# Six shared gather buffers and three raw weight buffers instead of five and four, in a two-layer hybrid trunk with product-key experts

## The chip, the cores and the metric

The kernel runs on one core of one Trainium2 chip. The metric is the device time of one execution in microseconds (us). A core has five engines that run at the same time, each with its own list of instructions in a fixed order: TensorE (PE) does matrix products, VectorE (DVE) and ScalarE (ACT) do elementwise work, GpSimd (POOL) issues the gathers, and SyncE (SP) issues nearly all plain transfers. An instruction that waits holds up all that stand behind it on its engine.

## The reference

Two layers work on 512 latent tokens and 256 context tokens of width 1024. Cut to what matters:

```python
for l in range(DEPTH):                      # 2
    p, pc = h @ w_in[l], hc @ w_in[l]       # latent, context
    ml_c, state = _mlstm_branch(pc, ...)    # context scan first
    ml_x, _ = _mlstm_branch(p, ..., state)  # its state starts the latent scan
    x = x + mod[2] * _mixer_merge(p, ml_x, ...)
    x = x + mod[5] * _peer(h, w_q, keys, u_tab, v_tab)
    # the context stream likewise, in layer 0 only

def _peer(h, ...):      # per token: 8 heads x 16 = 128 experts e, weights g
    a = gelu(einsum('nhkd,nd->nhk', u_tab[e], h)) * g
    return einsum('nhk,nhkd->nd', a, v_tab[e])
```

An expert is one row of `u_tab` and one row of `v_tab`, each 1024 numbers, in tables of 16384 rows a layer.

## The kernel before

**Weights.** Every weight tile of 128 x 1024 numbers (512 KB) comes from memory into a raw buffer `wr` (line 298 in `wload`, 817 in `routing`, 1138 in `s_block`). ScalarE casts it to `wh` (L292) and VectorE takes the difference `wl` (L293), after which the raw buffer is free; TensorE then makes three products for each pair (L312). The pool is opened once with `W_MIX`, (4, 3): four raw buffers and three of each part, for the whole kernel. In the context routing of layer 0 the raw tile goes to TensorE directly (L819), with no parts.

**Experts of the latent tokens.** In `peer_lat`, three of four token blocks use all experts as dense products (`s_block` and `dense`, accumulated on L1201). The fourth gathers rows: `gather` takes 128 rows of u and then 128 of v (one row for each of 128 tokens per gather, 512 KB), and VectorE reduces them (L948, L966). A row is read `LAG` rows after its gather was written down. These gathers are also tied to the pace of the dense loop.

**Experts of the context tokens.** In `gather_ctx`, each of four half blocks (64 tokens) takes 64 rows of u, reduced by VectorE on L1027, and 64 gathers of v, two for a step, whose products TensorE makes on L1061; these steps run one step behind their gathers (`VLAG`). A half block of v also holds one buffer for a matrix `dg` of its weights (L1055). The half blocks are spread as background work over the latent mixer of layer 0 (u of half 0, then v of half 0 with u of half 1 in alternation, then u of half 2), the routing of `peer_lat` of layer 0 (v of halves 1 and 2), and the start of layer 1 (u and v of half 3).

**Buffers of the rows.** All gathered rows use the tag `gat` with `GB` buffers (five), except the rows of u in the latent mixer of layer 0, which have a pool of their own, `ug`, with `UB` (three) and the distance `ULAG` (two). Three staging tiles of the context routing and the results also pass through `gat`. `rows` (line 916 on) picks the pool by its argument `own`.

**Order.** A background list hands out one row for so many microseconds of foreground work (`tick`). A scheduler then fixes each engine's order from its own estimate of when an instruction's inputs and buffers are ready, so a change in buffers also moves instructions that have nothing to do with gathers.

Of the kernel before, what the change touches and what calls it, by code (L numbers as in the profile page):

```python
# [47 lines left out]
V_COST, PS_C = 0.6, (3, 2)  # L48
NFT = 4
ND = 3  # L50
W_MIX = (4, 3)
NADA, ADA_RATE, ADA_RATE2 = 4, 0.3, 0.8
VB = 4
LAG = 3
COST_T = (2.0, 4.0)
GB = 5
UB, ULAG, VLAG = 3, 2, 1
GTB, VRB, GRB, GSB = 2, 2, 2, 2
AB, AHEAD = 3, 3

# [1 line left out]
def build(nc, tc, I, out):  # L62
# [126 lines left out]
    def mk(p, shape, dt=F32, tag=None, bufs=None):  # L189
        nid[0] += 1  # L190
        kw = {} if bufs is None else {"bufs": bufs}
        return p.tile(list(shape), dt, name=f"{tag}_{nid[0]}", tag=tag, **kw)

    def psum(tag="mm", n=None):
        p, t, bufs = pspool[tag]
        return mk(p, [128, 512], F32, t, bufs)
# [718 lines left out]
    def rows(tab, ix, own=False):  # L915
        t = mk(pu[0], [128, D], F32, "ug", UB) if own else mk(pg[0], [128, D], F32, "gat", GB)
        d = G.indirect_dma_start(out=t, out_offset=None, in_=tab, in_offset=bass.IndirectOffsetOnAxis(ap=ix, axis=0))  # L917
        if gate[0] is not None:
            tc.add_manual_dep(d.ins, gate[0].ins.name, SYNC, reason="spread the gathers over the loop")
        return t  # L920

    def gather(l, h, b, i12, gw, mod, s):
# [17 lines left out]
        def u_rows():  # L940
            ts = {}
            for j in range(128 + LAG):
                if j < 128:
                    ts[j] = rows(u_tab, eu[:, j:j + 1])
                if j >= LAG:
                    i = j - LAG
                    t = ts.pop(i)
# [6 lines left out]
        def v_rows(x):  # L954
            ts = {}
            on = mk(pg[0], [128, D], F32, "hn", 1)
            for j in range(128 + LAG):
                if j < 128:
                    ts[j] = rows(v_tab, eu[:, j:j + 1])
                if j >= LAG:  # L960
                    i = j - LAG
                    t = ts.pop(i)
# [14 lines left out]
    def gather_ctx(l, h, b, i12, gw, hnd, ond):  # L977
# [3 lines left out]
        u_tab, v_tab = I["peer_u"], I["peer_v"]  # L981
# [7 lines left out]
        def two(ps, src, c):  # L989

            for p in (0, 64):
                PE.matmul(ps[p:p + 64, :64], ident[:, 64 * c:64 * c + 64], src[:, p:p + 64], start=True, stop=True,
                          tile_position=(0, p))
            return ps[:, :64]

        def half(c):
            t0 = 128 * b + 64 * c
            i = 2 * b + c
            p = (pg[0], pl)[b]
            eu, a, w = (mk(p, [128, 64], dt, n + str(i), 1) for n, dt in (("hu", I32), ("ha", F32), ("hw", F32)))  # L1000
            V.tensor_scalar(eu, two(psum("sm"), ef, c), float(l * 16384), None, op0=ALU.add)
            V.tensor_copy(w, two(psum("sm"), gw, c))
            hn = mk(pg[0], [128, D], F32, "hn" if i == 0 else "gat", 1 if i == 0 else GB)
            for k in range(KT):
                ps = psum("sm")
                for q in (0, 64):
                    PE.matmul(ps[q:q + 64, :128], h[k][0][:, t0:t0 + 64], ident, start=True, stop=True,
                              tile_position=(0, q))
                S.copy(hn[:, 128 * k:128 * k + 128], ps[:, :128])
            if i:  # L1010
                nc.gpsimd.dma_start(hnd[i - 1], hn)

            def u_rows():
                hx = hn
                if i:
                    hx = mk(pg[0], [128, D], F32, "hn", 1)
                    nc.gpsimd.dma_start(hx, hnd[i - 1])
                ts = {}
                own = pu[0] is not None
                lag = ULAG if own else LAG  # L1020
                for j in range(64 + lag):
                    if j < 64:
                        ts[j] = rows(u_tab, eu[:, j:j + 1], own)
                    if j >= lag:
                        n = j - lag
                        t = ts.pop(n)
                        V.scalar_tensor_tensor(t, t, 1.0, hx, op0=ALU.mult, op1=ALU.mult, accum_out=a[:, n:n + 1])  # L1027
                    if j < 64:
                        yield
                S.activation(a, a, AF.Gelu_apprx_tanh)  # L1030
                V.tensor_tensor(a, a, w, ALU.mult)
                ps = psum("acc")
                for q in (0, 64):
                    PE.matmul(ps[q:q + 64, :64], a[q:q + 64, :], ident[q:q + 64, q:q + 64], start=True, stop=True,
                              tile_position=(q, q))
                S.copy(at[:, 64 * c:64 * c + 64], ps[:, :64])

            def v_rows():
                po = psum("acc")
                ts = {}  # L1040
                for p in range(32 + VLAG):
                    if p < 32:
                        ts[p] = []
                        for q in range(2):
                            tok = 64 * c + 32 * q + p
                            ts[p].append(rows(v_tab, ev[:, tok:tok + 1]))
                            if q == 0:
                                yield
                    if p >= VLAG:
                        n = p - VLAG  # L1050
                        rg, r = n // 16, n % 16
                        if r == 0:

                            dg = mk(pg[0], [128, 2, 16, 32], F32, "gat", GB)
                            G.memset(dg, 0.0)  # L1055
                            dd = dg.rearrange("p q r c -> p q (r c)")[:, :, 16 * rg:16 * rg + 15 * 33 + 1:33]
                            V.tensor_copy(dd, at[:, 64 * c:64 * c + 64].rearrange("p (q r) -> p q r", q=2)
                                          [:, :, 16 * rg:16 * rg + 16])
                        t = ts.pop(n)
                        for m in range(4):  # L1060
                            PE.matmul(po[32 * m:32 * m + 32, :], dg[:, m % 2, r, :],  # L1061
                                      t[m % 2][:, 512 * (m // 2):512 * (m // 2) + 512],
                                      start=n == 0, stop=n == 31, tile_position=(0, 32 * m))
                    if p < 32:
                        yield
                on = mk(pg[0], [128, 512], F32, "gat", GB)
                S.copy(on, po)
                nc.gpsimd.dma_start(ond[i], on)

            return u_rows, v_rows  # L1070

        return half(0) + half(1)

    def add_ctx(x, i, src, mod):

        on = mk(pg[0], [128, 512], F32, "gat", GB)
        nc.gpsimd.dma_start(on, src)
# [69 lines left out]
    def dense(l, h, gd, sp, nsp, nb, x, mod):  # L1147
# [62 lines left out]
        for b in range(nb):  # L1210
            on.append(mk(pg[0], [128, D], F32, "gat", GB))
            for half in range(2):
# [52 lines left out]
    def weight_pool(nr=0, ns=0):  # L1265

        pt.close()
        if pw_cm[0]:
            pw_cm[0].__exit__(None, None, None)
            pw_cm[0] = None  # L1270
        if nr:
            pw_cm[0], pw[0] = open_pool("pw", "right")
            pw[1:] = [nr, ns]
            pt.open()
# [13 lines left out]
    def ctx_residual(src):  # L1288
        cm, p = right_pool("xc")
        x = mk(p, [128, KT, CTX], F32, "xc")  # L1290
        nc.sync.dma_start(x, src.rearrange("(k p) t -> p k t", p=128))
        return x, cm
# [32 lines left out]

    weight_pool(*W_MIX)
    xc, xc_cm = ctx_residual(I["ctxT"])
# [246 lines left out]
```

## Time and profile before

| | us |
|---|---|
| three runs | 4578.3, 4589.01, 4588.94 |
| their median | 4588.94 |
| the profiled execution | 4592.53 |
| its span in the trace | 4590.7 |
| TensorE busy in it | 4241.2 |
| TensorE idle in it (4590.7 less 4241.2) | 349.5 |

The profile is of one execution. Around its span lie 1.8 us. It ran 3.6 us longer than the median of the three runs. TensorE's busy time includes time at a lower granted clock; the granted clock is 1.0 at full speed.

### The profile page before, as it was taken

How to read it: one execution, taken by the hardware profiler on the slowest of the kernel's cores; microseconds unless marked ns; L12 is line 12 of the kernel's file. 1: busy time of each engine (PE TensorE's matmuls, PEld its weight loads, DVE VectorE, ACT ScalarE, POOL GpSimd, SP SyncE). 2: the span in 40 equal slices, each digit the busy share in tenths (PEclk: the TensorE clock that was granted, in tenths of full speed). 3: DMA queues.
4: the chain of work that ended last, by engine and by line, in shares of the span. 5: the costliest groups of instructions: out<-in, count | busy, mean ns of one | idle time of the engine just before them, and what ended most of it. 6: DMA issues, size and time to landing. Idle time of an engine off the chain costs nothing.

```text
span 4590.7 us, 61300 instructions
## 1 busy us (share of the span) xinstructions
PE 4241.2 (92%) x22364; PEld 3459.9 (75%) x22364; DVE 3319.5 (72%) x6764; ACT 1628.8 (35%) x2314; POOL 1302.9 (28%) x1061
## 2 busy tenths in 40 slices
PE   7899769987999999999999888989999999999998
PEld 4795545655667799788888764567789998888887
DVE  3854878766578497677777685365699996777775
ACT  3541212322324355333333331243335553333333
POOL 0000346552243331233333354200012322233231
PEclk8999859988999999999999999989999999999999
DMA  7546768986577896999999787512248889898984
GB/s 279 202 152 221 261 210 319 342 282 205 183 271 253 305 344 241 339 323 319 326 333 326 255 288 252 199 60 74 92 151 295 314 297 328 300 313 310 312 313 157
DMA packets 417342, 1187.42 MB, mean 259 GB/s; under 512 B 39440, under 2 KB 142608, under 8 KB 413968
## 3 DMA queue, kind: packets, MB, share of 16 engines
q1 hardware_dynamic: 260992, 631.52, 39.9%
q0 software_dynamic: 150928, 549.52, 33.6%
q8 instruction: 176, 2.88, 0.3%
q10 hardware_dynamic: 5120, 2.47, 0.2%
q14 instruction: 126, 1.03, 0.1%
HBM read 1092.40 MB, written 90.96 MB: 258 GB/s over the span
## 4 chain that ended last, share of the span: by engine, by line
PE 37%; issue 15%; DMA 10%; DVE 9%; POOL 4%; ACT 1%; SPq 0%; POOLq 0%; DVEq 0%; ACTq 0%
PE s L312 11%; PE acc L1201 11%; PE mm L312 9%; POOL gat L917 4%; DMA gsr<-sp 3%; DMA vr<-in_peer_v 2%; DMA gat<-in_peer_v,ev 2%; PE sm L1120 2%; DMA gat<-in_peer_v,eu 1%; DVE gat L948 1%; DMA gat<-in_peer_u,eu 1%; DVE wl L293 1%; DVE vl L293 1%; DVE hn L966 1%; PE acc L1061 1%
## 5 line engine op out<-in xcount | busy, mean ns | idle before, releaser
L292 ACT CAST wh<-wr 128x1024 fp32r<-128x1024 f32 x498 | 521.6, 1048 | 1234.9 <-PE mm L312 706.9
L293 DVE TENSOR_TENSOR wl<-wr,wh 128x1024 fp32r<-128x1024 f32 x498 | 608.0, 1221 | 347.8 <-ACT wh L292 343.0
L312 PE MATMUL s<-hh,wh 128*128 128x384 f32 x2048 | 702.1, 343 | 3.8 <-ACT gs L1144 3.8
L312 PE MATMUL s<-hh,wl 128*128 128x384 f32 x2048 | 694.6, 339 | 5.0 <-DVE wl L293 5.0
L312 PE MATMUL s<-hl,wh 128*128 128x384 f32 x2048 | 693.7, 339 | 0.0
L917 POOL DMA_INDIRECT gat<-in_peer_u,eu x256 | 332.9, 1300 | 1258.5 <-DVE pu L861 468.3
L312 PE MATMUL mm<-hh,wh 128*128 128x512 f32 (+1 forms) x1552 | 592.7, 384 | 42.0 <-DVE sg L787 19.8
L1201 PE MATMUL acc<-vh,al 128*128 128x512 f32 x1536 | 605.2, 394 | 14.0 <-DVE al L293 13.9
L312 PE MATMUL mm<-hh,wl 128*128 128x512 f32 (+1 forms) x1552 | 588.4, 380 | 30.7 <-DVE wl L293 30.5
L1201 PE MATMUL acc<-vl,ah 128*128 128x512 f32 x1536 | 604.7, 394 | 7.7 <-DVE vl L293 7.7
L1201 PE MATMUL acc<-vh,ah 128*128 128x512 f32 x1536 | 602.2, 393 | 10.0 <-ACT vh L292 5.4
L312 PE MATMUL mm<-hl,wh 128*128 128x512 f32 (+1 forms) x1552 | 586.8, 379 | 3.7 <-DVE hl L293 2.3
L917 POOL DMA_INDIRECT gat<-in_peer_v,eu x256 | 335.2, 1309 | 643.8 <-PE acc L1201 485.2
L292 ACT CAST vh<-vr 128x1024 fp32r<-128x1024 f32 x256 | 268.8, 1050 | 545.0 <-DMA vr<-in_peer_v 521.7
L917 POOL DMA_INDIRECT gat<-in_peer_v,ev x256 | 301.7, 1179 | 477.0 <-PE acc L1061 352.4
L312 PEld LDWEIGHTS mm<-hh,wh 128*128 128x128 f32 x1552 | 306.3, 198 | 147.0 <-issue 52.9
L312 PEld LDWEIGHTS s<-hh,wh 128*128 128x128 f32 x2048 | 386.6, 189 | 30.5 <-issue 14.1
L312 PEld LDWEIGHTS s<-hh,wl 128*128 128x128 f32 x2048 | 386.1, 189 | 6.1 <-DVE wl L293 6.0
L966 DVE SCALAR_TENSOR_TENSOR hn<-gat,a,hn 128x1024 f32<-128x1024 f32 x254 | 325.6, 1282 | 89.8 <-DMA gat<-in_peer_v,eu 89.3
L312 PEld LDWEIGHTS s<-hl,wh 128*128 128x128 f32 x2048 | 386.7, 189 | 4.3 <-issue 0.8
L312 PEld LDWEIGHTS mm<-hh,wl 128*128 128x128 f32 x1552 | 306.4, 197 | 110.8 <-DVE wl L293 39.2
L293 DVE TENSOR_TENSOR vl<-vr,vh 128x1024 fp32r<-128x1024 f32 x256 | 313.0, 1223 | 98.6 <-ACT vh L292 98.1
(378 smaller groups left out, 7005.5 us busy)
## 6 DMA issues: line engine op xcount, KB each, us to landing
wr<-in_peer_uT SPq DMA_DIRECT2D x256, 512.0 KB, 5.2
vr<-in_peer_v SPq DMA_DIRECT2D x256, 512.0 KB, 5.9
wr<-in_w_inT SPq DMA_DIRECT2D x134, 512.0 KB, 4.5
wada<-in_w_adaT SPq DMA_DIRECT2D x96, 512.0 KB, 4.5
gd<-gt SPq DMA_DIRECT2D x24, 2048.0 KB, 8.2
gr<-gd SPq DMA_DIRECT2D x64, 768.0 KB, 8.8
sp<-gs SPq DMA_DIRECT2D x78, 384.0 KB, 4.8
gsr<-sp SPq DMA_DIRECT2D x78, 384.0 KB, 6.2
```

Of the source, the lines that this page charges most:

```text
L292: S.copy(hi, src)
L293: V.tensor_tensor(lo, src, hi, ALU.subtract)
L312: PE.matmul(ps, w[k][a], x[k][b], start=first and k == 0 and i == 0, stop=last and k == n - 1 and i == 2)
L917: d = G.indirect_dma_start(out=t, out_offset=None, in_=tab, in_offset=bass.IndirectOffsetOnAxis(ap=ix, axis=0))
L948: V.scalar_tensor_tensor(t, t, 1.0, hn, op0=ALU.mult, op1=ALU.mult, accum_out=a[:, i:i + 1])
L966: V.scalar_tensor_tensor(on, t, a[:, i:i + 1], on, op0=ALU.mult, op1=ALU.add)
L1061: PE.matmul(po[32 * m:32 * m + 32, :], dg[:, m % 2, r, :], t[m % 2][:, 512 * (m // 2):512 * (m // 2) + 512], start=n == 0, stop=n == 31, t ...
L1120: PE.matmul(ps[:, 128 * i:128 * i + 128], o2[:, i].rearrange("p a b -> p (a b)"), o1[:, i, :], start=True, stop=True)
L1201: mm = PE.matmul(acc[b][half], a[p][:, ts], v[q][:, ds], start=done == 0 and n == 0, stop=done == 127 and n == 2)
```

## The change

Five numbers and one condition are changed. The raw weight buffers go from four to three, the buffers of `gat` from five to six (4 KB per partition either way). The distance `LAG` goes from three to four rows, `ULAG` from two to three. In the latent mixer of layer 0, every fourth row of u (index 3, 7, 11 and so on) takes a buffer of `gat`, the other three take the pool `ug` as before.

```diff
--- before.py
+++ after.py
@@ -48,13 +48,13 @@
 V_COST, PS_C = 0.6, (3, 2)
 NFT = 4
 ND = 3
-W_MIX = (4, 3)
+W_MIX = (3, 3)
 NADA, ADA_RATE, ADA_RATE2 = 4, 0.3, 0.8
 VB = 4
-LAG = 3
+LAG = 4
 COST_T = (2.0, 4.0)
-GB = 5
-UB, ULAG, VLAG = 3, 2, 1
+GB = 6
+UB, ULAG, VLAG = 3, 3, 1
 GTB, VRB, GRB, GSB = 2, 2, 2, 2
 AB, AHEAD = 3, 3
 
@@ -1020,7 +1020,7 @@
                 lag = ULAG if own else LAG
                 for j in range(64 + lag):
                     if j < 64:
-                        ts[j] = rows(u_tab, eu[:, j:j + 1], own)
+                        ts[j] = rows(u_tab, eu[:, j:j + 1], own and j % (ULAG + 1) < UB)
                     if j >= lag:
                         n = j - lag
                         t = ts.pop(n)
```

No transfer, product or reduction is added or removed: there are 1065 instructions on GpSimd and 1163 on SyncE in both. What moves is shown below at three places. The number behind a name counts the tiles in program order, and one tile can be a number or two apart in the two kernels; `hu_888` and `hu_902` are the row numbers of u of half blocks 0 and 1, `ev` those of v.

GpSimd in the latent scan of layer 0, before. Every row of u goes in turn through the three `ug` buffers, with the first v rows and the first `dg` between them:

```order
L917 DMA ug_5434<-in_peer_u,hu_888_4613 128x1024
L917 DMA gat_5761<-in_peer_v,ev_885_4608 128x1024
L917 DMA ug_5437<-in_peer_u,hu_888_4613 128x1024
L917 DMA ug_5440<-in_peer_u,hu_888_4613 128x1024
L917 DMA ug_5443<-in_peer_u,hu_888_4613 128x1024
L1055 MEMSET gat_5763 128x1024
L917 DMA ug_5446<-in_peer_u,hu_888_4613 128x1024
L917 DMA ug_5449<-in_peer_u,hu_888_4613 128x1024
L917 DMA ug_5499<-in_peer_u,hu_888_4613 128x1024
L917 DMA ug_5502<-in_peer_u,hu_888_4613 128x1024
L917 DMA ug_5505<-in_peer_u,hu_888_4613 128x1024
L917 DMA ug_5508<-in_peer_u,hu_888_4613 128x1024
```

The same place after:

```order
L917 DMA ug_5436<-in_peer_u,hu_888_4613 128x1024
L917 DMA gat_5501<-in_peer_u,hu_888_4613 128x1024
L917 DMA ug_5439<-in_peer_u,hu_888_4613 128x1024
L917 DMA gat_5513<-in_peer_u,hu_888_4613 128x1024
L917 DMA gat_5564<-in_peer_u,hu_888_4613 128x1024
L917 DMA ug_5445<-in_peer_u,hu_888_4613 128x1024
L917 DMA ug_5448<-in_peer_u,hu_888_4613 128x1024
L917 DMA ug_5498<-in_peer_u,hu_888_4613 128x1024
L917 DMA gat_5623<-in_peer_u,hu_888_4613 128x1024
L917 DMA gat_5635<-in_peer_u,hu_888_4613 128x1024
L917 DMA ug_5504<-in_peer_u,hu_888_4613 128x1024
L917 DMA gat_5686<-in_peer_u,hu_888_4613 128x1024
```

Rows of u in `gat` (5501, 5513, 5564, 5623, 5635, 5686) now stand up to several rows ahead of their turn; the v rows come later.

GpSimd at the start of the alternation of v of half 0 and u of half 1, before:

```order
L917 DMA ug_5758<-in_peer_u,hu_902_4657 128x1024
L917 DMA ug_5809<-in_peer_u,hu_902_4657 128x1024
L917 DMA gat_5812<-in_peer_v,ev_885_4608 128x1024
L917 DMA ug_5814<-in_peer_u,hu_902_4657 128x1024
L917 DMA gat_5817<-in_peer_v,ev_885_4608 128x1024
L917 DMA ug_5823<-in_peer_u,hu_902_4657 128x1024
L917 DMA gat_5826<-in_peer_v,ev_885_4608 128x1024
L917 DMA ug_5890<-in_peer_u,hu_902_4657 128x1024
L917 DMA gat_5893<-in_peer_v,ev_885_4608 128x1024
L917 DMA ug_5899<-in_peer_u,hu_902_4657 128x1024
```

And after:

```order
L917 DMA gat_5808<-in_peer_u,hu_902_4657 128x1024
L917 DMA gat_5811<-in_peer_v,ev_885_4608 128x1024
L917 DMA gat_5816<-in_peer_v,ev_885_4608 128x1024
L917 DMA ug_5813<-in_peer_u,hu_902_4657 128x1024
L917 DMA gat_5825<-in_peer_v,ev_885_4608 128x1024
L917 DMA ug_5822<-in_peer_u,hu_902_4657 128x1024
L917 DMA ug_5889<-in_peer_u,hu_902_4657 128x1024
L917 DMA gat_5892<-in_peer_v,ev_885_4608 128x1024
L917 DMA gat_5898<-in_peer_u,hu_902_4657 128x1024
L917 DMA gat_5901<-in_peer_v,ev_885_4608 128x1024
```

One row of u in four now takes its place among the v rows' buffers.

SyncE in the context routing of layer 0 (`wr` are the raw tiles of the query weights, `wada` those of the modulation of layer 1, which wait for a product of this routing), before:

```order
L817 DMA wr_3634<-in_w_qT 128x1024
L817 DMA wr_3672<-in_w_qT 128x1024
L817 DMA wr_3710<-in_w_qT 128x1024
L248 DMA wada_3606<-in_w_adaT 128x1024
L248 DMA wada_3608<-in_w_adaT 128x1024
L248 DMA wada_3644<-in_w_adaT 128x1024
L248 DMA wada_3646<-in_w_adaT 128x1024
L817 DMA wr_3748<-in_w_qT 128x1024
L817 DMA wr_3786<-in_w_qT 128x1024
L248 DMA wada_3682<-in_w_adaT 128x1024
L248 DMA wada_3684<-in_w_adaT 128x1024
```

And after:

```order
L817 DMA wr_3634<-in_w_qT 128x1024
L817 DMA wr_3672<-in_w_qT 128x1024
L248 DMA wada_3606<-in_w_adaT 128x1024
L248 DMA wada_3608<-in_w_adaT 128x1024
L248 DMA wada_3644<-in_w_adaT 128x1024
L248 DMA wada_3646<-in_w_adaT 128x1024
L817 DMA wr_3710<-in_w_qT 128x1024
L817 DMA wr_3748<-in_w_qT 128x1024
L248 DMA wada_3682<-in_w_adaT 128x1024
L248 DMA wada_3684<-in_w_adaT 128x1024
L817 DMA wr_3786<-in_w_qT 128x1024
```

Each raw tile behind the third now stands one or two `wada` pairs later, since its buffer is that of the tile three before it.

## Rows read from the trace of the kernel before

**Rows 1.** The page: span, and busy time, share and instructions of each engine.

```profile
span 4590.7 us, 61300 instructions
...
PE 4241.2 (92%) x22364; PEld 3459.9 (75%) x22364; DVE 3319.5 (72%) x6764; ACT 1628.8 (35%) x2314; POOL 1302.9 (28%) x1061
```

**Rows 2.** Stage windows: stretch, length, busy (count) per engine, PEclk, DMA share, GB/s.

```profile
560.00:700.00 140.00, 83.46 (x420) 62.98 (x420) 103.99 (x225) 34.74 (x76) 57.70 (x53) 0.62 0.65 210
1380.00:1610.00 230.00, 216.32 (x1303) 175.65 (x1303) 150.38 (x378) 88.64 (x114) 81.63 (x66) 0.96 0.79 281
1800.00:2600.00 800.00, 777.62 (x3716) 677.19 (x3716) 603.65 (x757) 279.38 (x385) 269.08 (x210) 0.99 0.90 317
2760.00:3000.00 240.00, 214.10 (x1035) 132.51 (x1033) 106.40 (x167) 53.31 (x76) 77.90 (x74) 0.93 0.63 214
```

**Rows 3.** Waits of VectorE, 560:700: waiter, releaser, total us, times, longest.

```profile
DVE ug L1027 <- DMA ug<-in_peer_u,hu: 18.1, 15, 4.9
```

**Rows 4.** Waits of TensorE, 560:700.

```profile
PE sm L541 <- DVE nt L537: 12.1, 2, 10.1
```

**Rows 5.** VectorE in order of time: start, length, instruction, idle before it.

```profile
582.71 1.23 DVE L1027 SCALAR_TENSOR_TENSOR ug<-ug,hn 128x1024 f32<-128x1024 f32 x1 [4.88 <-DMA ug<-in_peer_u,hu]
...
648.10 1.23 DVE L1027 SCALAR_TENSOR_TENSOR ug<-ug,hn 128x1024 f32<-128x1024 f32 x1 [0.55 <-DMA ug<-in_peer_u,hu]
```

**Rows 6.** Waits of VectorE in 700:1120 and of TensorE in 690:1035.

```profile
DVE ug L1027 <- DMA ug<-in_peer_u,hu: 69.8, 46, 4.2
...
PE mm L312 <- DVE sg L787: 11.0, 2, 7.1
```

**Rows 7.** TensorE's waits for v rows in 1035:1380, 1380:1610, 2760:3000.

```profile
PE acc L1061 <- DMA gat<-in_peer_v,ev: 4.8, 7, 2.3
...
PE acc L1061 <- DMA gat<-in_peer_v,ev: 13.6, 5, 4.2
...
PE acc L1061 <- DMA gat<-in_peer_v,ev: 17.2, 10, 4.3
```

**Rows 8.** GpSimd in order of time, two v rows of one step, 1526:1546.

```profile
1528.71 1.41 POOL L917 DMA_INDIRECT gat<-in_peer_v,ev  x1 [4.51 <-PE acc L1061]
1530.42 0.94 POOL L917 DMA_INDIRECT gat<-in_peer_v,ev  x1 [0.30 <-issue]
```

**Rows 9.** Waits of VectorE in 1800:2600 and 3800:4560, of TensorE in 1800:2600.

```profile
DVE hn L966 <- DMA gat<-in_peer_v,eu: 41.2, 24, 4.8
...
DVE hn L966 <- DMA gat<-in_peer_v,eu: 48.1, 25, 4.6
...
PE acc L1201 <- DVE al L293: 9.4, 9, 2.2
```

**Rows 10.** DMA issues: transfer, queue, count, KB each, median us to landing.

```profile
gat<-in_peer_v,ev POOLq DMA_INDIRECT x256, 6.0
...
ug<-in_peer_u,hu POOLq DMA_INDIRECT x192, 5.7
```

**Rows 11.** DMA issues in 36:115 and in 115:335.

```profile
wr<-in_w_inT SPq DMA_DIRECT2D x12, 512.0 KB, 7.0
...
wr<-in_w_inT SPq DMA_DIRECT2D x32, 512.0 KB, 3.6
```

**Rows 12.** Waits of ScalarE over the span; waits of SyncE in 36:335.

```profile
ACT wh L292 <- DMA wr<-in_peer_uT: 4.7, 1, 4.7
...
SPq L248 <- PE acc L252: 50.9, 16, 6.9
```

**Rows 13.** ScalarE in order of time, casts of context weights.

```profile
313.76 1.05 ACT L292 CAST wh<-wr 128x1024 fp32r<-128x1024 f32 x1 [1.55 <-PE mm L312]
...
317.36 1.05 ACT L292 CAST wh<-wr 128x1024 fp32r<-128x1024 f32 x1 [2.27 <-PE mm L312]
```

**Rows 14.** The weight casts and differences over the span: busy, mean ns, idle before.

```profile
L292 ACT CAST wh<-wr 128x1024 fp32r<-128x1024 f32 x498 | 521.6, 1048 | 1234.9 <-PE mm L312 706.9
...
L293 DVE TENSOR_TENSOR wl<-wr,wh 128x1024 fp32r<-128x1024 f32 x498 | 608.0, 1221 | 347.8 <-ACT wh L292 343.0
```

## The prediction

> **What bounds the kernel now.** I read the page first, for the engine that is busy most. TensorE is, 4241.2 of 4590.7 us [rows 1], so a gain has to come out of its 349.5 idle us, or out of time at a lower clock. Then the windows by stage, to see where the idle time lies: 56.5 us of it stand in the 140 us of the latent scan (560:700), where the granted clock is 0.62, a mean between the two levels of 1.2 and 2.4 GHz; 13.7 in 1380:1610, 25.9 in 2760:3000, and only 22.4 in the 800 us of the dense stretch of layer 0 [rows 2]. Then the waits in those stretches, to see what ends the idle time. In the scan TensorE waits for VectorE (12.1 us for one operand) [rows 4], which itself waits 18.1 us in 15 pieces for gathered rows of u [rows 3]. Where v rows of the context run, TensorE waits for the rows themselves: 4.8, 13.6 and 17.2 us, 22 waits in all [rows 7]; in 1380:1610 that is all its idle time. So the kernel is bound by TensorE nearly everywhere, and by the gathers in a few known places. The buffer that is given up lies on another path, that of the weights.
>
> **The u rows in the scan: -10 us.** The change lets a row of u be gathered three rows ahead of its use instead of two, and GpSimd's new order runs rows in `gat` further ahead still. Nothing is added; VectorE's reductions stay where they were within some three rows. Most waits there look like 0.55 us, a row that lands just too late; one is 4.88 us [rows 5], behind two copies of staging tiles in GpSimd's queue, and I leave that one. The other 14 are 13.2 us (18.1 less 4.9). Reductions there come every 2 to 3 us, so a third row of lead covers all of them. VectorE's chain sets the pace here, since TensorE is idle 40% of the stretch, but part of what comes earlier will meet waits for TensorE, so I take 10 of 13.2. Bounds: 0 and -18.
>
> **The u rows beside the merge: -3 us.** In 700:1120 VectorE waits 69.8 us for rows of u, but TensorE waits only 11.0 us for the product that VectorE makes of the gates [rows 6]; the rest is hidden by TensorE's own work. I take a quarter of the 11.0. A row of u now also sits among the v rows of half 0, whose buffers are thereby no more than before (six less one). If such a row has to wait for a v product, all gathers behind it on GpSimd wait too, the `ug` rows first, then VectorE. Bounds: +8 (one such wait of 1 us for every second one of the 16 shared rows of that half block) and -10 (nearly all of the 11.0).
>
> **The v rows of halves 1, 2 and 3: -18 us.** With five buffers, one holds `dg` and four hold rows: the two gathers of a step wait for the product two steps back, and the second starts 1.71 us after the first [rows 8]. With a fifth row buffer the first gather of a step takes a buffer that came free a step earlier, so only the second is left to issue when the last product ends, and it starts some 1.7 us earlier. Each wait is cut by that or vanishes: 5 x 1.7 = 8.5 of the 13.6 us; of the 17.2 us (10 waits of 1.7 on the mean, some longer) about 12; of the 4.8 us (7 waits) all. That is 25 if nothing else is late. Gathers land in 6.0 us on the median [rows 10], and with more in flight I expect that to grow, so I take 18. TensorE has its next work ready and is the bound there, so the whole of it should reach the end. Bounds: 0 and -25.
>
> **The dense stretches: -8 us.** With `LAG` four, a row is read half a dense block later. VectorE waits 41.2 us for rows of v in the first stretch and 48.1 in the second; TensorE waits 9.4 us for the operand `al` that VectorE makes [rows 9], of 22.4 idle us. Most of VectorE's wait is covered by operands prepared three blocks ahead. I take a third of the 22.4. The gathers here follow TensorE's pace, so the buffer gives them nothing. Bounds: 0 and -20.
>
> **The raw weight buffer: +8 us.** No transfer is added, but each raw tile can start only when the tile three before it is split, not four. In the latent stages a tile serves TensorE so long that nothing shows: in the whole span ScalarE's casts wait for a raw tile of the dense part once, 4.7 us [rows 12], and otherwise for a part buffer, that is for TensorE (706.9 us) [rows 14]. The context mixer is the narrow place. A slot's round there is a landing, a cast of 1.05 us, a difference of 1.22 [rows 14], and I count 0.33 for the issue (an estimate from transfer to transfer on SyncE). With a landing of 3.6 us [rows 11] that is 6.2 us, and three slots give a tile every 2.1 us, where TensorE takes one in 3.6 [rows 13] (the shortest, with no gate product, in 2.9). At 7.0 us, as in the first 115 us [rows 11], it is 9.6 us and a tile every 3.2 us: no longer clear of 2.9. Twelve tiles by 0.3 us are 4 us. SyncE also stands in `wada` issues for products of the modulation, 50.9 us in 16 waits [rows 12], with raw tiles behind it that have less lead now: another 4. In the context routing a raw tile goes behind one or two more `wada` pairs, but it still starts when the tile three before it is done, two tiles of TensorE work ahead; nothing. Bounds: -5 (modulation tiles go ahead of raw tiles in the new order, and TensorE waits for some of those) and +25.
>
> **Sum.** -10 - 3 - 18 - 8 + 8 = -31 us. Against the profiled execution's own 4592.5 that is 4561.5; the median of the runs lies 3.6 lower, so I give 4558. The bounds add to -78 and +33, and not all ends come together. The new order of instructions everywhere else has no sign that I can read; it widens the range by some 10 us on either side.
>
> **A page against the trace.** VectorE does wait for rows read two reductions after their gather, with landings of 5.7 us on the median [rows 10]. The Trainium skill, "DMA: Bandwidth & Descriptors", section "Anatomy of one DMA — SWDGE (gpsimd) path", fits a gather-path transfer as 2.0 us plus its bytes over 436 GB/s, 3.2 us for 512 KB (an estimate by that page). By it a lead of two rows would suffice, all gains above would be near zero, and the sum would be +8. The trace has 5.7 to 6.0 us and the waits, and I go by it.
>
> **Rivals.**
> - *No change, 4585.* The transfers are the limit, not the buffers: the DMA engines are busy 0.90 in the dense stretch and 0.79 in 1380:1610 [rows 2]. Then more rows in flight only land later. Of the sum, half of the v rows' 18 us stays (their waits come singly, with idle DMA time between), and the +8: -1, and with a little lost or won elsewhere 4575 to 4600. This also covers the case that the sixth buffer does not do what it says, being held by rows of u or by tiles taken early. Against it: in 560:700 the DMA engines are busy only 0.65. The same skill page, section "Queues, rings and completion order", says that each DMA engine takes turns packet by packet between the queues that have work; by that a fuller gather queue would slow the weight loads, which would push towards this rival.
> - *Slower, 4610.* The three-slot ring binds in the context mixer. It decides from a landing (with the wait in SyncE's queue) above 3 x 3.6 - 2.6 = 8.2 us. If SyncE's stands of 3 us on the mean (50.9 over 16) come on top of 7.0, a round is 12.6 us and a tile every 4.2 instead of 3.6: 0.6 us for some 60 tiles is 36 us. With the gains at half (-15), 4589 + 21 = 4610. Against it: medians of 3.6 us after 115 us [rows 11].
> - *Larger gain, 4520.* In the scan the shorter waits also lift the clock above 0.62, so that the small products on VectorE's chain come sooner: 20 us more of the 56.5 idle; the v rows give all 25 and the dense stretches 15. That is -65 to -70.
>
> **How the numbers follow.** Forecast (own range 4535 to 4575) 0.50, larger gain 0.15, no change 0.20, slower 0.15. A comparison of this kernel can tell about 0.3% from no change, 14 us: faster is below 4575, slower above 4603. So faster 0.65, same 0.20, slower 0.15. For 8 in 10 I reach into the larger gain at 4512 and into the slower case at 4606.
>
> **What would show it.** Right: the waits for v rows in 1380:1610 and 2760:3000 fall from 30.8 us to about 14; VectorE's wait for u rows in the scan from 18 to about 6, with the scan some 10 us shorter; ScalarE's casts still wait for TensorE and not for raw tiles. Wrong: landings of gathers that rise by 2 us or more (no change), casts or TensorE waiting for raw tiles before 335 us (slower), or a scan whose length stays although VectorE's waits are gone, which would mean that its chain runs through TensorE.

## The result and the profile after

| | before | after |
|---|---|---|
| median of four runs, us | 4583.62 (4574.84 to 4589.01) | 4503.34 (4492.59 to 4523.19) |
| the profiled execution, us | 4592.53 | 4504.02 |
| its span, us | 4590.7 | 4502.3 |
| TensorE idle in it, us | 349.5 | 293.9 |

The ratio is 0.9837, with a 95% interval of 0.9815 to 0.9858: about 80 us or 1.6% faster. I had said 4558 in a range of 4512 to 4606. The sign was right and the size was not: the measured time lies below the whole range, and below the larger-gain rival's 4520 too.

The page of the kernel after, span and busy times, answers to [rows 1]. VectorE's work is the same (3319.5 and 3319.1 us). Of the 88.4 us between the two spans, TensorE's idle time gives 55.6 and its busy time 32.8.

```profile
span 4502.3 us, 61268 instructions
...
PE 4208.4 (93%) x22364; PEld 3447.4 (77%) x22364; DVE 3319.1 (74%) x6764; ACT 1624.5 (36%) x2312; POOL 1304.6 (29%) x1061
```

**Where the time went.** To read a change that moves instructions, I cut both traces at the same events (the last product or result of a stage) and compared the lengths of the stages. A stage can hold some products more or fewer, since the order differs; neighbours are then read together.

| stage (before, us) | before | after | change | changed kernel once more |
|---|---|---|---|---|
| context mixer, modulation, first query weights (0 to 452) | 452.2 | 448.5 | -3.7 | +2.2 |
| context routing (452 to 567) | 114.5 | 105.9 | -8.6 | -8.0 |
| latent scan (to 718) | 151.6 | 142.3 | -9.3 | -8.9 |
| merge, first part (to 808) | 89.3 | 88.5 | -0.8 | -1.2 |
| merge, convolution (to 1057) | 249.1 | 234.3 | -14.8 | -21.9 |
| last products of the latent mixer (to 1177) | 120.6 | 106.3 | -14.3 | -11.4 |
| latent routing, v of halves 1 and 2 (to 1851) | 673.2 | 666.4 | -6.8 | -10.7 |
| dense stretch of layer 0 (to 2613) | 762.9 | 759.9 | -3.0 | -9.7 |
| start of layer 1, u and v of half 3 (to 2985) | 371.5 | 353.8 | -17.7 | -11.5 |
| rest of layer 1 (to 4573) | 1587.7 | 1578.6 | -9.1 | -1.2 |

The last column is a second measurement of the changed kernel in its own profiled execution (below); it shows how far one stage scatters, up to 8 us. Two places carry the gain: the first latent mixer with the routing ahead of it (452 to 1177 us before), 725.1 us before and 677.3 after, and the start of layer 1.

Two of these stages in both kernels, as windows (stretch, length, busy time and count of PE, PEld, DVE, ACT, POOL, then granted clock, DMA share, GB/s). Before:

```profile
807.60:1056.70 249.10, 207.93 (x942) 141.95 (x941) 174.07 (x283) 65.20 (x89) 134.59 (x116) 0.92 0.86 306
1056.70:1177.30 120.60, 106.84 (x436) 83.52 (x435) 68.24 (x97) 33.02 (x43) 24.51 (x19) 0.93 0.55 181
```

After:

```profile
785.20:1019.50 234.30, 204.88 (x941) 140.44 (x940) 174.71 (x285) 60.08 (x85) 144.59 (x116) 0.93 0.91 328
1019.50:1125.80 106.30, 102.75 (x436) 81.27 (x435) 66.22 (x95) 33.09 (x43) 20.76 (x17) 0.99 0.59 193
```

The counts of products agree (942 and 941, 436 and 436), so these are the same stages. TensorE's idle time falls from 41.2 to 29.4 us in the first and from 13.8 to 3.5 in the second. In the second its busy time falls as well, 106.8 to 102.8, with the clock at 0.99 in place of 0.93.

**What VectorE and TensorE wait for.** The waits of VectorE after, in the scan (556:672, answering to [rows 3]) and behind it (672:1087.5, to [rows 6]); waiter, releaser, total, times, longest:

```profile
DVE ug L1027 <- DMA ug<-in_peer_u,hu: 4.7, 4, 3.1
...
DVE ug L1027 <- DMA ug<-in_peer_u,hu: 40.4, 31, 4.2
...
DVE gat L1027 <- DMA gat<-in_peer_u,hu: 4.8, 3, 3.5
```

In the scan 18.1 us have become 4.7; behind it 69.8 have become 45.2 for both pools together. Over the whole stretch the sum was 98.5 us before and is 54.6 now. TensorE's wait for the gates' product in 672:1087.5 is now

```profile
PE mm L312 <- DVE sg L787: 5.8, 2, 4.1
```

**Why the rows came late.** GpSimd in order of time, in the last products of the mixer before (start, length, instruction, idle time before it and its releaser), and what VectorE met there:

```profile
1065.26 1.68 POOL L917 DMA_INDIRECT ug<-in_peer_u,hu  x1 [2.00 <-DVE ug L1027]
1068.19 1.15 POOL L917 DMA_INDIRECT ug<-in_peer_u,hu  x1 [1.25 <-DVE ug L1027]
1069.94 0.94 POOL L917 DMA_INDIRECT ug<-in_peer_u,hu  x1 [0.60 <-DVE ug L1027]
1072.41 1.68 POOL L917 DMA_INDIRECT ug<-in_peer_u,hu  x1 [1.54 <-DVE ug L1027]
...
1070.91 1.23 DVE L1027 SCALAR_TENSOR_TENSOR ug<-ug,hn 128x1024 f32<-128x1024 f32 x1 [1.24 <-DMA ug<-in_peer_u,hu]
...
1080.93 1.23 DVE L1027 SCALAR_TENSOR_TENSOR ug<-ug,hn 128x1024 f32<-128x1024 f32 x1 [4.16 <-DMA ug<-in_peer_u,hu]
```

Each of these gathers starts when VectorE gives a buffer back, and VectorE then waits for a row of which the gather started too late: the reduction at 1070.91 for the gather of 1065.26, the one at 1080.93 for that of 1072.41. It is a circle of three buffers. GpSimd's side of it, in 718:1177 before, is the larger sign, and the prediction does not use it (the second line is its wait for buffers of v rows):

```profile
POOL ug L917 <- DVE ug L1027: 102.1, 54, 6.5
POOL gat L917 <- PE acc L1061: 32.1, 20, 4.8
```

The same stretch after (697:1126):

```profile
POOL ug L917 <- DVE ug L1027: 42.9, 25, 4.5
POOL gat L917 <- PE acc L1061: 40.2, 20, 6.1
...
POOL gat L917 <- DVE gat L1027: 11.2, 4, 8.2
```

**The v rows.** TensorE's waits for them after, in 1087:1547 (routing) and 2552:2906 (start of layer 1):

```profile
PE acc L1061 <- DMA gat<-in_peer_v,ev: 14.1, 7, 4.0
...
PE acc L1061 <- DMA gat<-in_peer_v,ev: 13.1, 7, 4.5
```

Before, the same stretches held 18.4 us in 12 waits and 17.2 in 10 [rows 7]. At the start of layer 1 the rows of u of half 3 use `gat` as well; VectorE's wait for them before (2613:2820) and after (2553:2740):

```profile
DVE gat L1027 <- DMA gat<-in_peer_u,hu: 21.4, 13, 7.2
...
DVE y L785 <- PE mm L312: 10.1, 1, 10.1
```

```profile
DVE gat L1027 <- DMA gat<-in_peer_u,hu: 11.7, 9, 4.8
```

**The weights.** In 0:343 after, TensorE waits for the two parts of weights as little as with four raw buffers (1.2 and 1.0 us):

```profile
PE mm L312 <- ACT wh L292: 1.2, 4, 0.3
...
PE mm L312 <- DVE wl L293: 1.0, 2, 0.7
```

ScalarE's casts do wait for raw tiles now: over the whole span for those of the dense part

```profile
ACT wh L292 <- DMA wr<-in_peer_uT: 43.0, 14, 5.0
```

where it was 4.7 us in one wait before [rows 12].

### The profile page after: what moved, and what is told of

Its sections match the earlier page's. It is cut to its first block, busy times and chain, and to the rows that moved or that the text cites. A ratio compares the mean times of both kernels' runs of the same rounds, so it can differ in the third digit from the quotient of the medians.

```text
span 4502.3 us, 61268 instructions
## 1 busy us (share of the span) xinstructions
PE 4208.4 (93%) x22364; PEld 3447.4 (77%) x22364; DVE 3319.1 (74%) x6764; ACT 1624.5 (36%) x2312; POOL 1304.6 (29%) x1061
## 4 chain that ended last, share of the span: by engine, by line
PE 32%; issue 19%; DMA 11%; DVE 9%; POOL 4%; ACT 1%; POOLq 0%; DVEq 0%; SPq 0%; ACTq 0%
PE mm L312 11%; PE s L312 9%; PE acc L1201 7%; POOL gat L917 4%; DMA gsr<-sp 3%; DMA vr<-in_peer_v 2%; PE sm L1120 2%; DMA gat<-in_peer_v,eu 2%; DMA gat<-in_peer_u,eu 1%; DVE wl L293 1%; DVE gat L948 1%; PE acc L1061 1%; DMA gat<-in_peer_v,ev 1%; DVE vl L293 1%; PE sm L828 1%
## 5 line engine op out<-in xcount | busy, mean ns | idle before, releaser
L917 POOL DMA_INDIRECT gat<-in_peer_v,eu x256 | 325.2, 1270 | 649.4 <-PE acc L1201 565.8
L312 PEld LDWEIGHTS mm<-hh,wh 128*128 128x128 f32 x1552 | 301.2, 195 | 127.4 <-issue 36.7
```

Source lines behind the costliest of these rows:

```text
L312: PE.matmul(ps, w[k][a], x[k][b], start=first and k == 0 and i == 0, stop=last and k == n - 1 and i == 2)
```

## Experiments

Each kernel is the kernel before with the edit shown. Ratios are to the kernel before; its median beside these runs was 4583.19, 4581.73 or 4580.11 us. Stage lengths are from one profiled execution each. "The stretch" is the one from 452 to 1177 us before, cut at the same events: 725.1 us before, 677.3 after. The execution of before was a long one (4592.53 us, where these medians are 4580 to 4583). With three raw buffers alone the stretch is 717.1 us, although VectorE waits no less for rows of u there (104.4 us in it); so up to 8 us of any difference from 725.1 below may be scatter.

### The price of the raw buffer alone

```diff
-W_MIX = (4, 3)
+W_MIX = (3, 3)
```

> The kernel before with three raw weight buffers instead of four, nothing else. Prediction's term: +8 us (up to +25), from the context mixer. Theory now (the gain comes from gathers, weights do not matter): within 5 us of the kernel before, and the context mixer up to 347 us as long as before or some 4 us shorter. Rival (the gain is a new order of instructions that fewer raw buffers bring about): 20 us or more faster.

Measured 4585.8 us (10 runs), ratio 1.0013 [0.9997, 1.0029]. The raw buffer costs nothing that can be told from zero, as the theory had it. TensorE's waits for parts in 0:347 are those of before; the largest wait there is for the modulation's own tiles, as before (18.3 us). ScalarE waits 37.5 us in 10 for raw tiles of the dense part, and the whole is no longer for it:

```profile
PE acc L252 <- DMA wada<-in_w_adaT: 19.2, 8, 11.1
...
PE mm L312 <- ACT wh L292: 1.2, 4, 0.3
```

### Six shared buffers alone, with LAG three and four

```diff
-W_MIX = (4, 3)
+W_MIX = (3, 3)
...
-GB = 5
+GB = 6
```

> Three raw weight buffers and six shared buffers, LAG three, rows of u in the first latent mixer as before. Theory: 15 to 25 us faster, at the v rows after 1140 us and at the start of layer 1, where the rows of u of half 3 and then v rows use the shared pool; LAG adds 10 to 15 us to it in the dense stretches. Rival (LAG is what shortens the start of layer 1): 5 to 10 us faster.

Measured 4549.37 us (4 runs), ratio 0.9919 [0.9897, 0.9941]. The stretch is 722.2 us, 2.9 below before, and neither side of the circle of u rows has shrunk (VectorE in 450:1172, GpSimd in 715:1172):

```profile
DVE ug L1027 <- DMA ug<-in_peer_u,hu: 99.6, 73, 6.0
...
POOL ug L917 <- DVE ug L1027: 119.3, 67, 5.0
```

Its gain, some 32 us and more than the theory's 15 to 25, is elsewhere: 20.5 us at the start of layer 1 and 8.0 in the latent routing. With `LAG` four in addition:

```diff
-W_MIX = (4, 3)
+W_MIX = (3, 3)
...
-LAG = 3
+LAG = 4
...
-GB = 5
+GB = 6
```

> Three raw weight buffers, six shared buffers, LAG four; rows of u in the first latent mixer as before (own pool of three, two ahead). Theory: 25 to 30 us faster, none of it between 450 and 1140 us: v rows of the context, start of layer 1, and a few us in the dense stretches. Prediction's terms give -18 -8 +8 = -18. Rival (order of instructions): the latent mixer of layer 0 gets shorter here too, by more than 20 us.

Measured 4548.17 us (5 runs), ratio 0.9929 [0.9907, 0.9952]: no difference from the kernel with `LAG` three, where the expectation above had 10 to 15 us for `LAG`. The stretch is 724.5 us, so nothing of the gain lies there. The dense stretch of layer 0 is 5.6 us shorter than before, and 6.6 with `LAG` three; it is also 6.2 shorter with three raw buffers alone, so that this looks like the scatter of the one execution of before.

### The u rows: three rows of lead from the pool's own buffers

```diff
-W_MIX = (4, 3)
+W_MIX = (3, 3)
...
-UB, ULAG, VLAG = 3, 2, 1
+UB, ULAG, VLAG = 4, 3, 1
```

> Three raw weight buffers; the freed buffer goes to the own pool of the rows of u (four buffers, rows three ahead); five shared buffers, LAG three, none of the rows of u in the shared pool. Theory (three rows of lead are what pays, whichever pool they are in): 45 to 55 us faster, all of it before 1140 us. Rival (the shared pool pays because rows of u run further ahead through it): 20 us faster or less.

Measured 4559.76 us (4 runs), ratio 0.9942 [0.9924, 0.9961]. Here `gat` keeps its five buffers. The whole is 23 us faster, which neither the theory (45 to 55) nor the rival (20 or less) had. The stretch is 688.4 us, 36.7 below before, but the latent routing is 9.2 us longer, for which I have no cause. VectorE's waits in the stretch (453:1142):

```profile
DVE ug L1027 <- DMA ug<-in_peer_u,hu: 54.5, 45, 5.9
```

So the fourth place for u rows by itself, with five buffers for v rows as before, carries two thirds to three quarters of the stretch's gain (36.7 of 47.8 and 51.4 us against before; 28.7 of 39.8 and 43.4 against three raw buffers alone).

### The shared form without LAG, and the whole change again

```diff
-W_MIX = (4, 3)
+W_MIX = (3, 3)
...
-GB = 5
-UB, ULAG, VLAG = 3, 2, 1
+GB = 6
+UB, ULAG, VLAG = 3, 3, 1
...
-                        ts[j] = rows(u_tab, eu[:, j:j + 1], own)
+                        ts[j] = rows(u_tab, eu[:, j:j + 1], own and j % (ULAG + 1) < UB)
```

> The changed kernel with the distance LAG back at three rows: three raw weight buffers, six shared buffers, rows of u in the first latent mixer three ahead, every fourth in the shared pool. Theory (VectorE's waits for rows of u in the first latent mixer lie on the path nearly in full): about 70 us faster than before, nearly the whole gain, with the start of layer 1 some 5 us longer than in the changed kernel. Rival (LAG and the ring of v rows carry the gain, as the prediction's terms had it): about 40 us faster or less.

Measured 4516.24 us (4 runs), ratio 0.9854 [0.9838, 0.9871]; the stretch is 682.8 us. That is 67 us faster, near the theory's 70 and far from the rival's 40. The changed kernel itself, measured a second time:

> The changed kernel once more beside these. Theory and rivals alike: 75 to 85 us faster than before; it is there so that the stages of a second profile of it show how far a stage's length varies between executions.

Measured 4510.94 us (4 runs), ratio 0.985 [0.9829, 0.9871]; the stretch is 673.7 us. It is 69 us faster, a little less than expected. The two intervals of the changed kernel and the one without `LAG` overlap, so whether `LAG` gives up to 10 us beside the other parts is not settled; alone it gave nothing.

### What the waits for u rows cost in all

In these kernels VectorE reduces a resident tile in place of the gathered row of u, into a scratch tile, in the latent mixer of layer 0. First the gathers still run, unread, through two buffers:

```diff
-UB, ULAG, VLAG = 3, 2, 1
+UB, ULAG, VLAG = 2, 2, 1
...
+                scr = mk(pu[0], [128, D], F32, "us", 1) if own else None
...
-                        V.scalar_tensor_tensor(t, t, 1.0, hx, op0=ALU.mult, op1=ALU.mult, accum_out=a[:, n:n + 1])
+                        if own:
+                            t = scr
+                        V.scalar_tensor_tensor(t, hx if own else t, 1.0, hx, op0=ALU.mult, op1=ALU.mult,
+                                               accum_out=a[:, n:n + 1])
```

> The kernel before, with the waits for rows of u of the first latent mixer taken away and the gathers kept: VectorE reduces a resident tile into a scratch tile in place of the gathered row (so the weights of these experts of the context are not the reference's), and the rows are still gathered, into two buffers that nobody reads. Theory (VectorE's 98.5 us of waits for these rows between 452 and 1139 us are on the path nearly in full): 60 to 95 us faster, all in that stretch. Rival (the waits are mostly covered, as the prediction had it, and the new order brought the gain): 10 to 25 us faster.

Measured 4592.14 us (10 runs), ratio 1.0022 [1.0006, 1.0037]: a spoilt experiment. With two buffers, GpSimd itself stood for the landing of the unread rows (450:1150), and the copies of staging tiles and the v rows behind them came late; the scan is 29.6 us longer than before (in a profiled execution that ran 20 us over the median of the ten).

```profile
POOL ug L917 <- DMA ug<-in_peer_u,hu: 254.3, 146, 6.0
```

The same without the 192 gathers of u:

```diff
-                        ts[j] = rows(u_tab, eu[:, j:j + 1], own)
+                        ts[j] = None if own else rows(u_tab, eu[:, j:j + 1], own)
```

> The same with the 192 gathers of rows of u of the first latent mixer left out as well. Theory: within 15 us of the run that keeps the gathers, since the waits and not the traffic are the price. Rival (the rows' 100 MB of traffic slow the weights and the rows of v in that stretch): 25 us or more faster than the run that keeps them.

Measured 4493.54 us (4 runs), ratio 0.9803 [0.9782, 0.9824]; the stretch is 638.2 us, 86.9 below before. By its words the rival came true, 99 us faster than the run that keeps the gathers, but that run was the spoilt one. This kernel takes away the waits and the traffic together, and most of GpSimd's work in the stretch. To part them, the unread rows got four buffers, paid for with two raw weight buffers:

```diff
-W_MIX = (4, 3)
+W_MIX = (2, 3)
...
-UB, ULAG, VLAG = 3, 2, 1
+UB, ULAG, VLAG = 4, 2, 1
```

> As the kernel that kept the gathers of the rows of u and reduced a resident tile instead (so these experts' weights are not the reference's), but with four buffers for the rows that nobody reads instead of two, so that GpSimd's queue does not stand waiting for them to land; two raw weight buffers make the room. Judged by stage, from 472 us on, since two raw buffers cost some 20 us before that. Theory (what pays is that VectorE does not wait; GpSimd's stalls of 254 us spoilt the run with two buffers): the stretch from the end of the context routing to the latent norm gets 45 us or more shorter than before. Rival (the traffic of the gathers is the price, as the run without gathers suggests): 15 us shorter or less.

Measured 4591.59 us (10 runs), ratio 1.0027 [1.0014, 1.0041], because two raw buffers cost at the start and in the routing of layer 1 (next section). The stretch is 675.6 us: 49.5 below before, as the theory had it, and no shorter than with the change (677.3 and 673.7). Apart from scatter it is a lower bound of what VectorE's waits cost, since other waits are longer here. GpSimd still stood 65.1 us for landings, a quarter of the kernel with two buffers. TensorE waited 22.0 us for v rows in 720:1150, where it waits 4.0 with the change. And two raw buffers are felt in the stretch too: ScalarE stood 85.4 us for raw tiles in 474:1150, where it was 0.7 in the stretch before; most of it is

```profile
ACT wh L292 <- DMA wr<-in_w_inT: 60.5, 10, 19.1
```

So VectorE's waits cost at least some 50 us here (42 against three raw buffers alone) and, by the kernel without gathers, at most some 87 (79); the 47.8 (40) of the change are between a good half and nearly all of that. The convolution stage in the kernels with no gathers and with unread ones, as windows:

```profile
780.00:988.00 208.00, 194.02 (x935) 137.25 (x928) 193.72 (x317) 65.07 (x89) 44.89 (x35) 0.97 0.48 166
```

```profile
817.00:1046.00 229.00, 201.57 (x920) 139.55 (x919) 188.45 (x306) 64.83 (x88) 143.23 (x119) 0.92 0.93 342
```

208 against 229 us, with the DMA engines busy 0.48 and 0.93 and the clock 0.97 and 0.92. In the whole stretch the difference is 37 us. That the gathers cost this much beyond VectorE's waits is not shown: the transfers, GpSimd's time for them and its stalls are in the difference, and so are the raw buffers, four in the kernel without gathers and two in the other. These runs do not part them.

### Two raw buffers: where the slower rival decides

```diff
-W_MIX = (4, 3)
+W_MIX = (2, 3)
...
-UB, ULAG, VLAG = 3, 2, 1
+UB, ULAG, VLAG = 5, 4, 1
```

> Two raw weight buffers, five own buffers for the rows of u, four rows ahead, five shared buffers, LAG three. By stage. Theory (more lead removes more of VectorE's waits): the stretch from 452 us to the first row of u of the latent tokens is 10 us or more shorter than with four own buffers, and VectorE's waits for rows of u fall under 30 us. Rival (landings grow with the rows in flight, so that lead buys nothing further): within 5 us of four own buffers.

Measured 4598.2 us (10 runs), ratio 1.0032 [1.0016, 1.0048]. The stretch is 677.3 us, as with the change and 11.1 less than with four own buffers, as the theory had it. VectorE's waits in it (475:1152) are the least of all kernels that read their rows, though not under 30. Whether so much lead would bring more with three raw buffers is not shown:

```profile
DVE ug L1027 <- DMA ug<-in_peer_u,hu: 36.2, 26, 3.9
```

The loss is outside: 22.9 us by the end of the first 452 us, 28.9 in the latent routing of layer 1. Four own buffers with six shared ones:

```diff
-W_MIX = (4, 3)
+W_MIX = (2, 3)
...
-LAG = 3
+LAG = 4
...
-GB = 5
-UB, ULAG, VLAG = 3, 2, 1
+GB = 6
+UB, ULAG, VLAG = 4, 3, 1
```

> Two raw weight buffers, six shared buffers, LAG four, four own buffers for the rows of u, three rows ahead, none of them in the shared pool. By stage. Theory (the shared pool's rows that run ahead give what four own buffers do not): from the end of the context routing to the first row of u of the latent tokens it is 5 to 15 us longer than the changed kernel. Rival (only the count of buffers matters): as long or shorter, since nothing is shared. The whole is slower than the changed kernel by the 20 us that two raw buffers cost in the context mixer.

Measured 4585.4 us (10 runs), ratio 1.0011 [1.0, 1.0022]; the stretch is 693.3 us, no better than with four own buffers and five shared ones (688.4). Against the change it is 16 and 20 us longer, the theory's way and a little beyond its 5 to 15; the whole is 74 to 82 us slower than the changed kernel, where 20 was expected. And the change with a seventh shared buffer in place of a second raw one:

```diff
-W_MIX = (4, 3)
+W_MIX = (2, 3)
...
-LAG = 3
+LAG = 4
...
-GB = 5
-UB, ULAG, VLAG = 3, 2, 1
+GB = 7
+UB, ULAG, VLAG = 3, 3, 1
...
-                        ts[j] = rows(u_tab, eu[:, j:j + 1], own)
+                        ts[j] = rows(u_tab, eu[:, j:j + 1], own and j % (ULAG + 1) < UB)
```

> The changed kernel with one more raw weight buffer given up: two raw weight buffers, seven shared buffers, LAG four, ULAG three. Theory (raw buffers do not matter above two, shared buffers still do): 10 to 20 us faster than the changed kernel. Rival (with two, a raw tile's round of 6 to 10 us over two slots is 3 to 5 us a tile and binds in the context mixer, where a tile is used in 2.9 to 3.6): the first 347 us grow by 20 us or more and the whole is no faster than the changed kernel.

Measured 4576.03 us (10 runs), ratio 0.9985 [0.997, 1.0]. The rival came true. The start is 19.3 us longer, the routing of layer 1 30.8. The stretch is 707.9 us, 31 and 34 longer than with the change (in a profiled execution that ran 16 us over the median of the ten), so that two raw buffers may cost there as well. SyncE's wait for a raw buffer in 0:347 before, and here, and then ScalarE's wait for raw tiles in 3350:3900 here, which before was 4.7 us in the whole span [rows 12]:

```profile
SPq L298 <- DVE wl L293: 87.5, 22, 13.5
```

```profile
SPq L298 <- DVE wl L293: 144.3, 42, 9.5
...
ACT wh L292 <- DMA wr<-in_peer_uT: 96.4, 30, 9.0
```

Two raw buffers bind; with three ScalarE waits for raw tiles, and it costs nothing that shows. The mechanism of the slower rival is real, one buffer further down. No kernel that does the whole work was faster than the changed one.

## Why the prediction was right or wrong

**What bounds the kernel: right, but read too narrowly.** The idle time of TensorE was the place to look, and the gathers were behind it. But I went by what TensorE waits for by name, and where VectorE is late by rows, TensorE waits for whatever VectorE makes next, under many names. That is read from the sums below and not shown wait by wait.

**The u rows beside the merge, -3 us: the step that failed.** The stages from the end of the scan to the end of the mixer fell by 29.9 us (0.8, 14.8 and 14.3). Two sentences of that step were wrong. "TensorE waits only 11.0 us" stopped at 1035; to the end of the mixer it is 19.8 us, and after it is 5.8. And "the rest is hidden by TensorE's own work": TensorE's idle time fell by 23.1 us there, 14.0 of it in these waits; the other 6.8 us are busy time of the same products, at a clock of 0.95 in place of 0.93. The last stage, 120.6 us before, is the clean case: VectorE's waits for rows fell from 17.9 to 3.3 us in its first 82 us, and those 82.0 us became 67.5, one for one (4.3 of the 14.5 us in TensorE's busy time, with the clock at 0.98 in place of 0.90). My floor of -10 for this term was "nearly all of the 11.0", a bound made from one named wait; VectorE's 69.8 us was the bound that the trace gave. The feared wait did not come: in 697:1126 no gather of a shared u row waited for a v product. The reverse came, four gathers of v rows that waited for VectorE to reduce a shared u row, 11.2 us in all. The waits of v rows for products, behind which all gathers stand, went from 32.1 to 40.2 us (34.1 the second time), and did not decide.

**The context routing: a term that was missing.** u rows already run there, and VectorE waited 10.6 us for them, now 4.6. Routing and scan are read together, since some 25 products moved from one into the other: -17.9 us, nearly all of it idle time of TensorE (79.4 to 62.0), against VectorE's 28.7 us of waits that became 9.3. **The scan, -10 us,** is right by itself (-9.3), with waits of 18.1 become 4.7, near the 6 that I named.

**The v rows, -18 us, with a part of it in each place.** The shared buffers alone brought some 34 us (0.9919 and 0.9929), but less by the mechanism that I gave. In the routing it is -6.8 us, against some 10 that the term held for halves 1 and 2. In both stretches together, which hold the 30.8 us that I said would fall to about 14, the waits fell from 35.6 us (22) to 27.2 (14): a good third of the waits is gone, but those that are left did not become shorter. At the start of layer 1 it is -17.7 us against some 9, and six shared buffers alone give it (20.5). The u rows of half 3 also use these buffers: VectorE's wait for them fell by 9.7 us and its wait for a product of TensorE from 10.1 to 2.2, while one for ScalarE rose from 2.5 to 6.3. I had no term for that.

**The dense stretches, -8 us:** -3.0 in the first and -6.0 in the second, and the runs show that this is not `LAG` (nothing with six shared buffers). The execution of before was some 6 us long in the first; the second took 731.4 to 739.4 us in the kernels with three raw buffers and `LAG` three, 732.5 to 738.3 with four. The term was too large; near zero is what the runs support.

**The raw weight buffer, +8 us:** zero (1.0013). The landing in 115:335 is 3.6 us after as before [rows 11], where by my own sum a ring of three has room, and TensorE's waits for parts in 0:343 did not grow. One sign that I gave came out the other way: the casts of the dense part do wait for raw tiles (43.0 us, 4.7 before), and it cost nothing that shows.

**The sum.** The parts as the runs show them: weights 0, six shared buffers -34, u rows in the shared pool -33 more (4549.4 to 4516.2), and 5 to 13 us for the whole change against that, within overlapping intervals. Measured twice, the change brings 69 to 80 us, where I had 31: 38 to 49 are missing. Some 20 of them lie in the u rows (-33 for -13), some 16 in the shared buffers (-34 for -18), and 8 in the raw buffer's price that did not come; the 8 of the dense stretches go the other way. That is 36, and the rest is not settled. The split depends on the order in which the parts are added: four own buffers for u rows, without a sixth shared one, brought 23 us and not 33.

**The rivals.** *No change*: landings did rise with more in flight, by 0.6 to 0.7 us for weights and `ug` rows and to 7.4 for the shared u rows, and not by 2; those of v rows did not (7.2 and 7.0). The gain was not eaten. Medians in the convolution stage, before (807:1057) and after (785:1019), with the share of the DMA engines 0.86 and 0.91:

```profile
wr<-in_w_inT SPq DMA_DIRECT2D x23, 512.0 KB, 6.5
...
ug<-in_peer_u,hu POOLq DMA_INDIRECT x77, 6.2
```

```profile
wr<-in_w_inT SPq DMA_DIRECT2D x22, 512.0 KB, 7.1
...
ug<-in_peer_u,hu POOLq DMA_INDIRECT x58, 6.9
...
gat<-in_peer_u,hu POOLq DMA_INDIRECT x24, 7.4
```

The rise of weights and u rows together, in one execution each, agrees with what the Trainium skill says in "DMA: Bandwidth & Descriptors", section "Queues, rings and completion order", of turns between queues. Its fit in the section "Anatomy of one DMA — SWDGE (gpsimd) path", an estimate of 3.2 us for such a gather, by which nothing was to be gained, is about half of these medians, and the measurement decides. *Slower*: not at three raw buffers, as above. *Larger gain*: nearest in size (4520), wrong in its means. The scan's clock stayed (0.67 and 0.68 over the stage), the waits for v rows fell by less and `LAG` gave nothing; the gain came beside the merge, where I had put 3 us.

**What stays open.** Why four own buffers (688.4 us in the stretch) are less than three own and a shared place (682.8, 677.3 and 673.7), at the same total of VectorE's waits (54.5 and 54.6): the order shows shared rows gathered further ahead, but no run separates that from the sixth `gat` buffer. Six shared buffers beside four own ones did not do better than four own ones, though with two raw buffers, which may have cost there too. And what the 37 us between the two kernels without VectorE's waits are.

## What to carry to other kernels

When a ring of buffers is short, read it from both sides: a gather engine that waits for a reader to give buffers back (102.1 us here) and a reader that waits for the gather (98.5 us) are one circle, and another buffer can cut it. Bound such a gain by the late engine's own waits over every stage in which the ring runs (here 98.5 us; they fell by 43.9 and the stretch by 47.8), and not by the one wait of the busiest engine that carries a fitting name. Price a buffer that is given up by its ring's round, and find the count at which it binds by taking one more: three raw buffers cost nothing here, two cost 19 to 31 us in each of two places.

## What the runs showed of the hardware

- Shorter stalls went with a higher clock in places. In the last stage of the mixer idle time of 13.8 us fell to 3.5, the granted clock rose from 0.93 to 0.99, and the same products took 4.1 us less. It is 0.98 to 1.00 in all ten profiled executions with more lead or without the waits, 0.93 to 0.95 in the four others. At the start of layer 1 (2613.4:2819.9 before) idle time fell from 42.8 to 32.1 us and the clock rose from 0.89 to 0.92. That is weaker: over all kernels it is 0.87 to 0.89 with five shared buffers and 0.89 to 0.92 with six or seven. In the scan, at 0.67 and 0.68, it did not rise although 18 us of idle time went, with 24 more products in it.
- In these kernels a gather into a buffer whose last gather has not landed holds GpSimd up until the landing, even if nothing reads the row: 254.3 us in 146 waits with a ring of two, 65.1 us in 61 with a ring of four.
- Without VectorE's waits, but with the transfers and two raw buffers, a stage took 229 us at a DMA share of 0.93 and a clock of 0.92, and 208 at 0.48 and 0.97 without the transfers and with four raw buffers. How much of that is the transfers is not shown.
